# Four single feed-forward products by halves of the tokens, and a fifth PSUM bank for each pair of products

## The chip, the cores and the metric

The kernel runs on one core of a Trainium2 chip. The core has TensorE (PE in the rows; its weight loads are PEld), VectorE (DVE), ScalarE (ACT), GpSimd (POOL) and SyncE (SP, here only a DMA queue). The metric is device time of one execution in microseconds. The kernel before took 2143.89 us (median of 3 runs, 2141.85 to 2143.91).

## What is computed

One step of a two-layer backbone over 640 tokens of width 1024 (128 context tokens and 512 latent ones). Each layer has a token-mixing sub-layer and a SwiGLU feed-forward; the change is in the feed-forward alone:

```python
h = rms_norm(x, g_pre[1]) * (1 + sc2) + sh2
g, u = jnp.split(h @ w_ffn_in_l, 2, axis=-1)      # 1024 -> 2 x 2816
x = x + g2 * rms_norm((silu(g) * u) @ w_ffn_out_l, g_post[1])
```

All matrices are float32. The kernel splits each operand into a high and a low part of a shorter float format and adds three products (high by high, high by low, low by high), so each float32 product is three matmuls.

## The kernel before

**Tokens and weights.** The normalised input `h` stands transposed in `hT_hi` and `hT_lo` (128 partitions x 8 blocks of the width x 640 tokens). Tokens come in five tiles of 128, t0 to t4. `cut` places them so that the first half of the columns holds t1, t2 and half of t0, the second half the rest of t0 with t3 and t4. The 2816 columns of gate and up weights are 22 blocks of 128 each: `fg` (gate) and `fu` (up), n = 0 to 21. A block of weights arrives in a raw tile `wraw` (four of them) and is split by ACT (`whi`, the high part) and then DVE (`wlo`, the rest) into one of three slots of 1024 columns, or into one of two extra tiles `walt`, which lie in the memory called `m0` and `m1` (`alt_slot` says who uses which). `split_all` splits whatever next block finds a free slot, at the point of the program where a slot comes free; so the order of each engine's queue is set when the program is written out.

**The hand-over from the output projection.** `out_proj` computes its second half token tile by token tile. As a tile's last product ends, `tail` queues its residual, norm, transposes on PE (into `ps_t`), scale and shift (L609 on DVE for one half of the width, L611 on ACT for the other), and the split into `hT_hi` (L630, ACT) and `hT_lo` (L631; DVE does the first four blocks of the width, POOL the last four). These steps are deferred by a virtual clock (`defer`, `DELAYS`), and `run_tasks` puts them into the queues between products.

**Single products.** The first two blocks of each kind (n = 0, 1) are plain products of 24 matmuls for each half of the tokens (L650 to L652). The list `seq` is fg0, fu0, fg1, fu1. Before the change the first three go by halves: first half of the tokens for all three, then t3 and t4 have to be ready (`run_tasks(GTOK[1])`), then the second half; fu1 follows with both halves. Each result is drained from PSUM: ACT takes Silu for a gate (L1543), DVE multiplies for an up block (L1545) and the product is split into `aT` (L1547 on ACT, L1548 on DVE).

**Sums and pairs.** The other blocks go two at a time by a scheme of seven products of half the width by half the tokens (`pair`, 12 matmuls of 320 columns each, L744) in place of eight. It needs four sums of token blocks, S1 to S4, which `sums` makes from the normalised tokens in `nt` while the single products run: additions on DVE and POOL (L701, L705), then a split by ACT (L719) and DVE (L721). S1 is written to `m1`, S3 to `m0`, S2 to `o32`, S4 over the first four blocks of the second half of `hT`. `SUMS_AT` sets when each of the eight steps is put into the queues. The products take, in order: a block of `hT`, S2, S1, a block of `hT`, S3, S4, a block of `hT`.

**PSUM in a pair.** Six banks (`mm`) go round. Product 0 writes p1, copied out by ACT (L753); product 1 writes p2, read by DVE (L757, `u2 = p2 + m1`); product 2 writes p3, copied by ACT (L761). Product 3 is then added into p1, product 4 into p2 and product 5 into p3, each after that reader; product 6 has p4. DVE takes p2 again (L767), then p3 (L771) and p4 (L776). While the pairs of a layer run, DVE also does a slow side job, the modulation vectors of the next rounds (`ada_side`, L501 and L503).

Places in the program are named below by time. In layer 0 the single products start at 641 us and the first pair at 677 us; in layer 1 the same stretch starts at 1695.8 us and 1731.7 us. Each layer has 20 pairs: 4, 8 and 8, with a piece of the output product of the feed-forward after each.

Of the kernel before, what the change touches and what calls it, by code (L numbers as in the profile page):

```python
# [13 lines left out]
OP = mybir.AluOpType  # L14
# [10 lines left out]
HALVES = ((0, 320), (320, 640))  # L25
# [8 lines left out]
ADA_MIX = ([(0, 2), (0, 3), (0, 4)], [(1, 3), (1, 4)])  # L34
ADA_FFN = ([(0, 5), (1, 0), (1, 1), (1, 2)], [(1, 5)])
FFN_PARTS = (6, 8, 8)
SUMS_AT = (0.1, 0.2, 2.0, 3.0, 4.0, 5.0, 9.0, 99.0)
SUM_START, SUM_DT, SUM_ROWS = 5.0, 2.9, 256
TICK = 2.5
ADA_DT, ADA_LAG = (8.0, 1.8), 3  # L40
# [53 lines left out]
class Weights:  # L94
# [33 lines left out]
    @staticmethod  # L128
    def alt_slot(key):


        l, kind, n = key[:3]
        if kind in ("wo", "fo"):
            k0 = 0 if kind == "wo" else DFF // 128 - FFN_PARTS[-1]
            k1 = 6 if kind == "wo" else DFF // 128 - 2
            return {(0, k1): 0, (1, k0): 1}.get(key[2:])
        return 0 if n == 0 and (kind == "fg" or kind == "uc" and l) else None

    @staticmethod
# [148 lines left out]
class Kernel:  # L288
# [390 lines left out]
    def sums(self, z, offsets):  # L679

        nc, fix = self.nc, self.fix
        zv = z.rearrange("p t (k c) -> p t k c", c=128)
        tiles = {}

        blocks = ((1, 0), (1, 1), (2, 0), (2, 1), (0, 0)), ((0, 1), (3, 0), (3, 1), (4, 0), (4, 1))
        vec, pool = nc.vector.tensor_tensor, nc.gpsimd.tensor_tensor

        def pieces(half, kh):  # L690

            ks = slice(4 * kh, 4 * kh + 4)
            return zv[:, 1 + 2 * half:3 + 2 * half, ks, :], zv[:, 0, ks, 64 * half:64 * half + 64]

        def block(half, kh, i):
            t, b = blocks[half][i]
            return zv[:, t, 4 * kh:4 * kh + 4, 64 * b:64 * b + 64]

        def within(out, x, y, op):
            for i, (o, a, b) in enumerate(zip(*(pieces(*w) for w in (out, x, y)))):  # L700
                (pool if i else vec)(o, a, b, op=op)  # L701

        def across(out, x, y):
            for i in range(5):
                (pool if i in (1, 3) else vec)(*(block(*w, i) for w in (out, x, y)), op=OP.subtract)  # L705

        def store(name, at, tag):
            if tag is None:
                hi, lo = (w[:, 0:4, 320:640] for w in (self.hT_hi, self.hT_lo))
            else:  # L710
                s = fix.tile([128, 2, 4, 320], F32R, name=name, tag=tag, bufs=1)
                hi, lo = s[:, 0], s[:, 1]
            tiles[name] = hi, lo
            c = 64 * at[0]
            dh, dl = ((w[:, :, c:c + 256].rearrange("p k (t c) -> p t k c", t=2), w[:, :, 256 - 4 * c:320 - 4 * c])
                      for w in (hi, lo))
            src = pieces(*at)
            for o, a in zip(dh, src):
                nc.scalar.activation(o, a, AF.Copy)  # L719
            for o, a, b in zip(dl, src, dh):  # L720
                vec(o, a, b.bitcast(F32), op=OP.subtract)  # L721

        a11, a12, a21, a22 = (0, 0), (0, 1), (1, 0), (1, 1)
        steps = (lambda: within(a22, a21, a22, OP.subtract), lambda: across(a21, a11, a21),
                 lambda: store("S1", a22, "m1"), lambda: across(a11, a22, a11),
                 lambda: store("S2", a11, "o32"), lambda: within(a12, a12, a11, OP.add),
                 lambda: store("S3", a21, "m0"), lambda: store("S4", a12, None))
        for dt, f in zip(offsets, steps):
            self.defer(dt, f, "sums")
        h = lambda kh, half: tuple(w[:, 4 * kh:4 * kh + 4, 320 * half:320 * half + 320] for w in (self.hT_hi, self.hT_lo))  # L730
        self.left = (lambda: h(0, 0), lambda: tiles["S2"], lambda: tiles["S1"], lambda: h(1, 0), lambda: tiles["S3"],
                     lambda: tiles["S4"], lambda: h(1, 1))

    def pair(self, key, evac):

        nc, W = self.nc, self.W
        self.tmp = self.tmp[1], self.tmp[0], self.tmp[2]
        m1, u2, m5 = self.tmp
# [11 lines left out]
        psum = lambda: self.psum("mm")[:, :320]  # L750
# [2 lines left out]
        nc.scalar.activation(m1, p1, AF.Copy)  # L753
        end(0)
        p2 = psum()
        product(1, p2, True, False)
        nc.vector.tensor_tensor(u2, p2, m1, op=OP.add)  # L757
        end(1)
        p3 = psum()
# [3 lines left out]
        product(3, p1, False, True)  # L763
        evac(0, p1, 0)
        end(3)
        product(4, p2, False, True)
        nc.vector.tensor_tensor(m1, p2, m1, op=OP.add)  # L767
        nc.gpsimd.tensor_tensor(m5, m5, m1, op=OP.subtract)  # L768
        end(4)
        product(5, p3, False, True)  # L770
# [748 lines left out]
    def ffn(self, l):  # L1519
        nc = self.nc  # L1520
# [3 lines left out]
        for p, nt in enumerate(FFN_PARTS):  # L1524
# [27 lines left out]
            if p == 0:  # L1552
                first = FFN_SINGLE
                seq = [(kind, n) for n in range(first) for kind in ("fg", "fu")]
                self.tmp = [self.fp.tile([128, 320], F32, name=f"tmp{i}") for i in range(3)]
                for g in range(2):
                    self.run_tasks(GTOK[g])
                    if g:
                        self.sums(self.z, SUMS_AT)
                    for kind, n in seq[:3]:  # L1560
                        self.proj((l, kind, n), g, evac(kind, n), 4, HALVES)
                self.W.alt.clear()
                for kind, n in seq[3:]:
                    self.proj2((l, kind, n), evac(kind, n), HALVES)
                self.run_tasks(("sums",))
                rounds = ADA_FFN[l]
                self.run_tasks(range(5))
# [177 lines left out]
```

## Time and profile before

| | |
|---|---|
| time, median of 3 | 2143.89 us |
| the profiled execution | 2143.28 us |
| its span, first to last instruction | 2141.5 us |
| PE busy | 2089.6 us (98%) |
| DVE busy | 1237.4 us (58%) |
| ACT busy | 912.8 us (43%) |
| mean granted clock of PE | 0.995 |

The profile lists for each instruction its start, its length, and the idle time of its engine just before it with what ended that. A matmul of 320 columns is shown with a length of 0.31 us, but the next one starts 0.147 us after it: they overlap, so gaps between starts are read, not lengths. The profiled execution was 1.8 us longer than its span.

### The profile page before, as it was taken

The numbers are of one execution on the slowest core, as the hardware profiler recorded it, in microseconds if no ns is written. First come the engines' busy times: TensorE is split into PE (matmuls) and PEld (weight loads), VectorE is DVE, ScalarE is ACT, GpSimd is POOL, SyncE is SP. The second block draws the span as 40 slices with busy tenths as digits, with TensorE's granted clock in tenths as the row PEclk, the third lists the DMA queues.
The fourth block names the chain that finished last, engine by engine and source line by source line (L and its number), as shares of the span: only waits on it lengthen the run. The fifth ranks groups of instructions, "written<-read, shape, count | busy, mean of one in ns | idle before, by whom it ended". The sixth has DMA issues, their size and how long they took to land.

```text
span 2141.5 us, 35955 instructions
## 1 busy us (share of the span) xinstructions
PE 2089.6 (98%) x13876; PEld 1939.6 (91%) x13876; DVE 1237.4 (58%) x2289; ACT 912.8 (43%) x1947; POOL 515.1 (24%) x783
## 2 busy tenths in 40 slices
PE   6999999999999999999999999999999999999998
PEld 4999999998879889889889999999988798998996
DVE  3555664553357777777466556555533676563663
ACT  3644453432245434235356445434423543541541
POOL 3121325452123100100142124354321320010012
PEclk9999999999999999999999999999999999999999
DMA  8555769894644565554535466798855244442443
GB/s 277 153 115 147 162 194 187 212 212 137 224 157 140 178 186 166 175 162 142 195 110 143 128 150 168 191 195 202 185 177 197 99 141 146 139 148 79 138 153 123
DMA packets 369803, 349.68 MB, mean 163 GB/s; under 512 B 16608, under 2 KB 294144, under 8 KB 369376
## 3 DMA queue, kind: packets, MB, share of 16 engines
q1 hardware_dynamic: 337040, 293.51, 43.8%
q0 software_dynamic: 32160, 53.63, 14.5%
q8 instruction: 109, 1.79, 0.3%
q14 instruction: 62, 0.51, 0.1%
q10 hardware_dynamic: 432, 0.25, 0.0%
HBM read 335.50 MB, written 95.72 MB: 201 GB/s over the span
## 4 chain that ended last, share of the span: by engine, by line
PE 60%; DVE 3%; ACT 2%; POOL 2%; issue 1%; DMA 1%; DVEq 0%; POOLq 0%; ACTq 0%; SPq 0%
PE ps_mm L744 20%; PE ps_mm L650 7%; PE ps_mm L651 7%; PE ps_mm L652 6%; PE ps_mm L1406 5%; PE ps_mm L1408 5%; PE ps_mm L1407 5%; PE ps_t L842 1%; PE ps_o L856 1%; DMA vbt<-in_c_cvb 1%; PE ps_s L815 1%; PE ps_s L816 1%; POOL hT_lo L631 1%; ACT whi L172 1%; DVE wlo L173 0%
## 5 line engine op out<-in xcount | busy, mean ns | idle before, releaser
L173 DVE TENSOR_TENSOR wlo<-wraw,whi 128x512 fp32r<-128x512 f32 (+1 forms) x453 | 408.3, 908 | 406.8 <-ACT whi L172 401.4
L650 PE MATMUL ps_mm<-hT_hi,whi 128*128 128x256 f32 (+2 forms) x1552 | 489.3, 315 | 1.5 <-DVE sg L1369 1.0
L652 PE MATMUL ps_mm<-hT_hi,wlo 128*128 128x256 f32 (+2 forms) x1552 | 480.9, 310 | 0.7 <-DVE wlo L173 0.7
L651 PE MATMUL ps_mm<-hT_lo,whi 128*128 128x256 f32 (+2 forms) x1552 | 480.6, 310 | 0.0
L172 ACT ACTIVATE whi<-wraw 128x512 fp32r<-128x512 f32 (+1 forms) x453 | 354.4, 790 | 287.2 <-PE ps_mm L1408 147.1
L650 PEld LDWEIGHTS ps_mm<-hT_hi,whi 128*128 128x128 f32 x1552 | 292.6, 189 | 11.5 <-issue 7.2
L652 PEld LDWEIGHTS ps_mm<-hT_hi,wlo 128*128 128x128 f32 x1552 | 292.1, 188 | 1.2 <-DVE wlo L173 1.2
L651 PEld LDWEIGHTS ps_mm<-hT_lo,whi 128*128 128x128 f32 x1552 | 292.5, 188 | 0.4
L744 PE MATMUL ps_mm<-S,whi 128*128 128x320 f32 x960 | 212.8, 309 | 5.6 <-DVE tmp L757 5.6
L768 POOL TENSOR_TENSOR tmp<-tmp,tmp 128x320 f32<-128x320 f32 x40 | 53.5, 1336 | 652.3 <-DVE tmp L767 608.7
L744 PE MATMUL ps_mm<-hT_hi,whi 128*128 128x320 f32 x640 | 198.0, 309 | 1.4 <-ACT tmp L753 1.4
L744 PE MATMUL ps_mm<-hT_hi,wlo 128*128 128x320 f32 x640 | 197.3, 308 | 0.0
L744 PE MATMUL ps_mm<-hT_lo,whi 128*128 128x320 f32 x640 | 197.3, 308 | 0.0
L744 PEld LDWEIGHTS ps_mm<-S,whi 128*128 128x128 f32 x960 | 160.1, 188 | 7.1 <-DVE tmp L757 7.1
L1406 PE MATMUL ps_mm<-whi,aT 128*128 128x512 f32 x400 | 158.4, 396 | 0.0
L1408 PE MATMUL ps_mm<-whi,aT 128*128 128x512 f32 x400 | 157.9, 395 | 0.0
L1407 PE MATMUL ps_mm<-wlo,aT 128*128 128x512 f32 x400 | 157.8, 394 | 0.0
L744 PE MATMUL ps_mm<-S,wlo 128*128 128x320 f32 x480 | 148.1, 309 | 0.0
L744 PEld LDWEIGHTS ps_mm<-hT_hi,whi 128*128 128x128 f32 x640 | 120.1, 188 | 3.5 <-ACT tmp L753 2.5
L650 PE MATMUL ps_mm<-o,whi 128*128 128x256 f32 (+1 forms) x384 | 121.1, 315 | 0.0
L744 PEld LDWEIGHTS ps_mm<-hT_lo,whi 128*128 128x128 f32 x640 | 120.2, 188 | 0.2
L744 PEld LDWEIGHTS ps_mm<-hT_hi,wlo 128*128 128x128 f32 x640 | 120.1, 188 | 0.0
(236 smaller groups left out, 3893.8 us busy)
## 6 DMA issues: line engine op xcount, KB each, us to landing
wraw<-in_w_in SPq DMA_DIRECT2D x92, 512.0 KB, 4.3
wraw<-wsum SPq DMA_DIRECT2D x160, 256.0 KB, 3.3
wsum<-in_w_ffn_in POOLq DMA_DIRECT2D x64, 512.0 KB, 7.8
wraw<-in_w_ffn_in SPq DMA_DIRECT2D x120, 256.0 KB, 3.4
wraw<-in_w_ada SPq DMA_DIRECT2D x56, 512.0 KB, 3.8
wraw<-in_w_ffn_out SPq DMA_DIRECT2D x44, 512.0 KB, 4.1
ada_side<-in_w_ada SPq DMA_DIRECT2D x40, 512.0 KB, 3.8
wsum<-in_w_ffn_in SPq DMA_DIRECT2D x32, 512.0 KB, 6.7
```

What stands on the lines that cost most here:

```text
L172: self.k.nc.scalar.activation(hi, src, AF.Copy)
L173: self.k.nc.vector.tensor_tensor(lo, src, hi.bitcast(F32), op=OP.subtract)
L631: (lo_on or (nc.gpsimd if q else nc.vector)).tensor_tensor(lo, zq, hi.bitcast(F32), op=OP.subtract)
L650: nc.tensor.matmul(ps, wh, xh[:, c0:c1], start=(k == 0), stop=False)
L651: nc.tensor.matmul(ps, wh, xl[:, c0:c1], start=False, stop=False)
L652: nc.tensor.matmul(ps, wl, xh[:, c0:c1], start=False, stop=(k == K - 1))
L744: nc.tensor.matmul(ps, w[p][:, k, :], x[q][:, k, :], start=first and k == 0 and j == 0, stop=last and k == 3 and j == 2, skip_group_check= ...
L768: nc.gpsimd.tensor_tensor(m5, m5, m1, op=OP.subtract)
L815: nc.tensor.matmul(out, u["q"][:, h, u["qc"]], u["khi"](h), start=True, stop=False)
L1406: nc.tensor.matmul(ps, xh, u.hi[:, i, :], start=st and i == 0, stop=False)
L1407: nc.tensor.matmul(ps, xh, u.lo[:, i, :], start=False, stop=False)
L1408: nc.tensor.matmul(ps, xl, u.hi[:, i, :], start=False, stop=sp and i == 1)
```

## The change

Three edits go together. All four single products now go by halves: fg0, fu0, fg1 and fu1 for the first half of the tokens, then all four for the second. fu0 is split into the second extra tile `walt`, in `m1`, and no longer into one of the three slots; S1 moves to `m0`, S3 to `m1`, and four times in `SUMS_AT` move back. And the pair's product 4 no longer adds into p2: it has a bank of its own, p5, and DVE computes `m1 = p5 + u2` instead of `p2 + m1` (the sum is the same). No instruction is added or dropped except that two splits of 1024 columns are now four of 512.

```diff
-SUMS_AT = (0.1, 0.2, 2.0, 3.0, 4.0, 5.0, 9.0, 99.0)
+SUMS_AT = (0.1, 0.2, 3.3, 4.0, 5.0, 6.0, 9.0, 99.0)
...
+        if n == 0 and kind == "fu":
+            return 1
         return 0 if n == 0 and (kind == "fg" or kind == "uc" and l) else None
...
-                 lambda: store("S1", a22, "m1"), lambda: across(a11, a22, a11),
+                 lambda: store("S1", a22, "m0"), lambda: across(a11, a22, a11),
                  lambda: store("S2", a11, "o32"), lambda: within(a12, a12, a11, OP.add),
-                 lambda: store("S3", a21, "m0"), lambda: store("S4", a12, None))
+                 lambda: store("S3", a21, "m1"), lambda: store("S4", a12, None))
...
         p2 = psum()
-        product(1, p2, True, False)
+        product(1, p2, True, True)
...
-        product(4, p2, False, True)
-        nc.vector.tensor_tensor(m1, p2, m1, op=OP.add)
+        p5 = psum()
+        product(4, p5, True, True)
+        nc.vector.tensor_tensor(m1, p5, u2, op=OP.add)
...
-                    for kind, n in seq[:3]:
+                    for kind, n in seq:
                         self.proj((l, kind, n), g, evac(kind, n), 4, HALVES)
                 self.W.alt.clear()
-                for kind, n in seq[3:]:
-                    self.proj2((l, kind, n), evac(kind, n), HALVES)
```

In the changed file the lines stand 2 or 3 further down (L609 is L611, L173 is L175, L719 is L721, L753 is L755).

The queue of DVE in layer 0, where the output projection hands over to the single products. `nt` holds the tokens, `ps_t` their transposes, and the rows from L609 (L611) on are those of tile t2. Before:

```order
L590 TENSOR_SCALAR nt<-x,ss 128x1024
L631 TENSOR_TENSOR hT_lo<-nt,hT_hi 128x4x128
L1513 TENSOR_TENSOR nt<-ps_mm,gm 128x512
L609 TENSOR_SCALAR nt<-ps_t,a_0_6195,sh_0_6032 128x128 x4
L1483 SCALAR_TENSOR_TENSOR x<-nt,ss,x 128x1024
L631 TENSOR_TENSOR hT_lo<-nt,hT_hi 128x4x128
L173 TENSOR_TENSOR wlo_272<-wraw,whi_271 128x1024
L173 TENSOR_TENSOR wlo_270<-wraw,whi_269 128x1024
L590 TENSOR_SCALAR nt<-x,ss 128x1024
L173 TENSOR_TENSOR wlo_268<-wraw,whi_267 128x1024
```

And of the changed kernel:

```order
L592 TENSOR_SCALAR nt<-x,ss 128x1024
L633 TENSOR_TENSOR hT_lo<-nt,hT_hi 128x4x128
L1516 TENSOR_TENSOR nt<-ps_mm,gm 128x512
L175 TENSOR_TENSOR walt<-wraw,walt 128x1024
L611 TENSOR_SCALAR nt<-ps_t,a_0_6195,sh_0_6032 128x128 x4
L1486 SCALAR_TENSOR_TENSOR x<-nt,ss,x 128x1024
L633 TENSOR_TENSOR hT_lo<-nt,hT_hi 128x4x128
L175 TENSOR_TENSOR wlo_272<-wraw,whi_271 128x1024
L175 TENSOR_TENSOR wlo_270<-wraw,whi_269 128x1024
L592 TENSOR_SCALAR nt<-x,ss 128x1024
L175 TENSOR_TENSOR wlo_268<-wraw,whi_267 128x512 x2
```

The split of fu0 has moved from one of the slots into `walt`, which is free earlier: it now stands in front of t2's scale and shift. The two halves at the end are the first two parts of the first pair.

The queue of ACT in layer 0 just ahead of the first pair (`aT` drains fu1; the rows `hT_hi<-nt` are S4; the first `tmp` row is the copy of product 0 out of p1, the second that of product 2 out of p3). Before:

```order
L1547 ACTIVATE aT_6640<-sg 128x320 x2
L172 ACTIVATE whi_267<-wraw 128x512 x2
L719 ACTIVATE hT_hi<-nt 128x2x4x128
L719 ACTIVATE hT_hi<-nt 128x4x64
L753 ACTIVATE tmp_6645<-ps_mm 128x320
L172 ACTIVATE whi_271<-wraw 128x512 x2
L761 ACTIVATE tmp_6646<-ps_mm 128x320
```

And of the changed kernel:

```order
L1550 ACTIVATE aT_6647<-sg 128x320
L174 ACTIVATE whi_269<-wraw 128x512 x2
L721 ACTIVATE hT_hi<-nt 128x2x4x128
L721 ACTIVATE hT_hi<-nt 128x4x64
L755 ACTIVATE tmp_6652<-ps_mm 128x320
L174 ACTIVATE whi_267<-wraw 128x512 x2
L763 ACTIVATE tmp_6653<-ps_mm 128x320
```

The order is the same, but only one drain of fu1 (its second half) stands here; the other has moved ahead of the sums, and PE has one half product less to do before the first pair.

## Rows read from the trace of the kernel before

**Rows 1.** The head of the page: the span, and the busy time of each engine.

```profile
span 2141.5 us, 35955 instructions
PE 2089.6 (98%) x13876; PEld 1939.6 (91%) x13876; DVE 1237.4 (58%) x2289; ACT 912.8 (43%) x1947; POOL 515.1 (24%) x783
```

**Rows 2.** The view of waits, PE alone: who waited for whom, us in total, times, longest.

```profile
PE ps_mm L744 <- DVE tmp L757: 5.6, 6, 1.3
...
PE ps_mm L650 <- ACT hT_hi L630: 4.1, 3, 1.9
```

**Rows 3.** The timeline of PE over the single products of layer 0 (start, length, idle before it and what ended it in brackets): the second matmul of the first half, the wait in the first half, the last matmul of the first half, the first of the second half, the thirteenth of it, the first of fu0 and of fg1 in the second half. The last row is layer 1's first matmul of the second half.

```profile
641.33 0.41 PE L651 MATMUL ps_mm<-hT_lo,walt 128*128 128x320 f32 x1
...
644.73 0.42 PE L651 MATMUL ps_mm<-hT_lo,walt 128*128 128x320 f32 x1 [1.38 <-POOL hT_lo L631]
...
655.19 0.31 PE L652 MATMUL ps_mm<-hT_hi,wlo 128*128 128x320 f32 x1
657.36 0.46 PE L650 MATMUL ps_mm<-hT_hi,walt 128*128 128x320 f32 x1 [1.85 <-ACT hT_hi L630]
...
661.11 0.31 PE L650 MATMUL ps_mm<-hT_hi,walt 128*128 128x320 f32 x1
...
662.87 0.31 PE L650 MATMUL ps_mm<-hT_hi,whi 128*128 128x320 f32 x1
...
666.39 0.31 PE L650 MATMUL ps_mm<-hT_hi,whi 128*128 128x320 f32 x1
...
1712.08 0.45 PE L650 MATMUL ps_mm<-hT_hi,walt 128*128 128x320 f32 x1 [1.85 <-ACT hT_hi L630]
```

**Rows 4.** The view of stretches, 658 to 661 us and 770.5 to 872 us (the eight pairs of layer 0's second part): start and end, length, then busy time of PE, PEld, DVE, ACT and POOL, PE's granted clock (0.5 is 1.2 GHz, 1.0 is 2.4 GHz), DMA share, GB/s.

```profile
658.00:661.00 3.00, 2.91 (x11) 2.92 (x12) 1.83 (x3) 0.02 (x1) 1.87 (x2) 0.50 0.00 0
770.50:872.00 101.50, 98.44 (x674) 96.59 (x673) 74.25 (x124) 49.26 (x100) 11.14 (x12) 1.00 0.57 167
```

**Rows 5.** The timeline of DVE around the first half: the low part of t2, a split of 1024 columns, and the low part of t4.

```profile
640.59 0.68 DVE L631 TENSOR_TENSOR hT_lo<-nt,hT_hi 128x512 fp32r<-128x512 f32 x1
...
646.34 1.22 DVE L173 TENSOR_TENSOR wlo<-wraw,whi 128x1024 fp32r<-128x1024 f32 x1
...
657.34 0.69 DVE L631 TENSOR_TENSOR hT_lo<-nt,hT_hi 128x512 fp32r<-128x512 f32 x1 [0.47 <-ACT hT_hi L630]
```

**Rows 6.** The timeline of POOL: its share of the low part of t2 and of t4.

```profile
640.23 4.45 POOL L631 TENSOR_TENSOR hT_lo<-nt,hT_hi 128x512 fp32r<-128x512 f32 x1 [1.95 <-ACT hT_hi L630]
...
657.90 1.27 POOL L631 TENSOR_TENSOR hT_lo<-nt,hT_hi 128x512 fp32r<-128x512 f32 x1 [4.29 <-ACT hT_hi L630]
```

**Rows 7.** The timeline of DVE through the sums: the first addition, the second (POOL works on its part at the same time), the last addition, the drain of fu0, four splits for the pair, S3's low part, the last drain of fu1.

```profile
659.20 1.75 DVE L701 TENSOR_TENSOR nt<-nt 128x1024 f32<-128x1024 f32 x1 [1.17 <-POOL hT_lo L631]
...
668.92 1.22 DVE L701 TENSOR_TENSOR nt<-nt 128x1024 f32<-128x1024 f32 x1
670.06 0.48 DVE L1545 TENSOR_TENSOR sg<-sg,ps_mm 128x320 f32<-128x320 f32 x1
...
671.60 2.66 DVE L173 TENSOR_TENSOR wlo<-wraw,whi 128x512 fp32r<-128x512 f32 x4
674.44 1.56 DVE L721 TENSOR_TENSOR S<-nt,S 128x1024 fp32r<-128x1024 f32 x2 [0.18 <-ACT S L719]
...
677.35 0.48 DVE L1545 TENSOR_TENSOR sg<-sg,ps_mm 128x320 f32<-128x320 f32 x1
```

**Rows 8.** The timeline of ACT from the last drain of fu1 to the copy out of p1.

```profile
677.86 0.47 ACT L1547 ACTIVATE aT<-sg 128x320 fp32r<-128x320 f32 x1 [0.95 <-DVE sg L1545]
...
679.28 1.34 ACT L719 ACTIVATE hT_hi<-nt 128x1024 fp32r<-128x1024 f32 x2
680.54 0.42 ACT L753 ACTIVATE tmp<-ps_mm 128x320 f32<-128x320 f32 x1
```

**Rows 9.** The timeline of PE: the first matmul of the first pair, and of its product 3.

```profile
676.95 0.31 PE L744 MATMUL ps_mm<-hT_hi,whi 128*128 128x320 f32 x1
...
682.23 0.31 PE L744 MATMUL ps_mm<-hT_hi,whi 128*128 128x320 f32 x1
```

**Rows 10.** The timeline of DVE in the first pair: the first step of the side job.

```profile
688.08 0.75 DVE L501 TENSOR_SCALAR ada_side<-ada_side,ada_st 128x1024 f32<-128x1024 f32 x1 [0.92 <-DMA ada_side<-in_w_ada]
```

**Rows 11.** The timeline of ACT: the copy out of p1 in the third pair of layer 0 and in the seventh.

```profile
706.43 0.42 ACT L753 ACTIVATE tmp<-ps_mm 128x320 f32<-128x320 f32 x1
...
802.08 0.42 ACT L753 ACTIVATE tmp<-ps_mm 128x320 f32<-128x320 f32 x1
```

**Rows 12.** The view of waits, PE alone, in two stretches: 770.5 to 872 us (the eight pairs of layer 0's second part) and 931.7 to 1034 us (its third part).

```profile
PE ps_mm L744 <- DVE tmp L757: 2.1, 2, 1.3
...
PE ps_mm L744 <- DVE tmp L757: 1.8, 2, 1.0
```

**Rows 13.** The timeline of PE: product 4 of the fifth pair, product 3 and product 4 of the seventh.

```profile
778.99 0.56 PE L744 MATMUL ps_mm<-S,whi 128*128 128x320 f32 x2 [1.29 <-DVE tmp L757]
...
802.55 0.41 PE L744 MATMUL ps_mm<-hT_hi,whi 128*128 128x320 f32 x1 [0.42 <-ACT tmp L753]
...
805.39 0.56 PE L744 MATMUL ps_mm<-S,whi 128*128 128x320 f32 x2 [0.82 <-DVE tmp L757]
```

**Rows 14.** The timeline of DVE in the fifth pair: the read of p2, and its next turn, after product 4.

```profile
778.45 0.49 DVE L757 TENSOR_TENSOR tmp<-ps_mm,tmp 128x320 f32<-128x320 f32 x1
...
781.06 0.49 DVE L767 TENSOR_TENSOR tmp<-ps_mm,tmp 128x320 f32<-128x320 f32 x1 [0.32 <-PE ps_mm L744]
```

## The prediction

> **What bounds the kernel now.** I read the page first, then PE's waits, then the timeline where they are. PE is busy 98% of the span [rows 1], so the change can give back only time in which PE waits or runs at half clock. The view of waits lists it [rows 2]: the two causes that the edits touch are the start of the second half of the tokens (PE on `hT_hi`, 4.1 us in three waits, two of them here) and product 4 of a pair (PE on L757, 5.6 us in six waits). The last matmul of the first half starts at 655.19 in layer 0 and the next one could start at 655.34, 0.147 us later. It starts at 657.36, and the thirteenth only at 661.11 [rows 3], for PE's granted clock has fallen to 0.5, which is 1.2 GHz of 2.4 [rows 4]. Thirteen matmuls on time would have reached 655.34 + 12 x 0.147 = 657.10, so the place costs 4.0 us. Layer 1 shows the same wait of 1.85 us [rows 3]. Elsewhere PE hardly waits for what is changed, so this is a matter of some 14 us in 2143.
>
> **Four products by halves, what it takes away.** A half product lasts 666.39 - 662.87 = 3.52 us [rows 3]. With fu1's first half put ahead of the second half, PE comes to t3 and t4 3.52 us later. The late operand is t4's low part, ready at 657.34 + 0.69 = 658.03 [rows 5] when PE would have wanted it at 655.34 + 0.15. POOL's share is ready at 657.90 + 1.27 = 659.17 [rows 6] and is wanted only by the second four blocks, 1.76 us after. So 2.7 us are missing, 3.52 are offered, the wait goes, and with it the fall of the clock: minus 4.0 us for each layer, if nothing comes after it.
>
> **What it adds ahead.** fu0's split into `walt` now stands in DVE's queue before t2's scale and shift (order above). DVE has no gap there; a split of 1024 columns takes 1.22 us [rows 5]. The low part of t2 ended at 640.59 + 0.68 = 641.27, and PE took it up at 641.33 [rows 3, 5]: no cover at all. So PE waits 1.2 us longer there. POOL's share of t2, after which the 1.38 us wait at 644.73 ends [rows 3, 6], follows the same scale and shift and moves by the same 1.2, so that wait keeps its length; the tails of t3 and t4 come behind it and move as well. ACT's half of the split costs nothing: ACT stood idle there for its next transposes. Plus 1.2 us for each layer. Bounds: 0 (the split fits a gap) and 1.2 + 1.9 (two waits so near each other lower the clock once more, priced like the fall above, 4.0 less its waits of 2.1). I take 1.2, since one wait of 1.38 did not lower it.
>
> **What comes late next.** PE would then begin the second half at 655.34 + 1.2 + 3.52 = 660.06 and the first pair after four halves, at 674.1, against 676.95 [rows 9]: 2.8 us earlier. But the sums wait for DVE, and DVE hardly gains. After t4 it now drains fu1's first half (ready on PE at 660.3; drain 671.60 - 670.06 = 1.54 us with ACT's turn in between), then does the chain from L701 to the drain of fu0, 670.06 - 659.20 = 10.86 us, less 0.6 because POOL's first piece is out of the way (1.75 against 1.22), then that drain (1.54), two splits (2.66 / 2), S3 (0.18 + 1.56), and the last drain's first step (0.48) [rows 7]: 16.9 us, to 677.2. Before, that step ended at 677.83. From there ACT drains, splits two parts, splits S4, and only then copies p1: 680.96 - 677.83 = 3.1 us [rows 7, 8]. So p1 is free at 680.3. PE wants to add product 3 into it at 674.1 + 3 x 1.76 = 679.4 and waits 0.9 us; S4 and the weights are ready in time. Product 3 of the first pair starts at 680.35 in place of 682.23 [rows 9]: of the 2.8 us, 1.9 are left. The Trainium skill ("SBUF — State Buffer", "Who interferes with whom") says that DVE with two SBUF inputs and a GpSimd instruction that reads SBUF exclude each other, and that the one that started second is blocked until the other ends. Rows agree in kind (POOL 1.27 alone, 4.45 beside DVE [rows 6]). If POOL alone were the one blocked in the sums, DVE's chain would be shorter and the 0.9 us wait would go, 1.8 us off the sum in both layers; the sum keeps the contended rows.
>
> **The bank for product 4.** Its wait for L757 goes. The third pair of each layer has one of 0.82 (what rows 12 and two pieces of that size leave of the 5.6), layer 0's later pairs 2.1 and 1.8 [rows 2, 12]. But PE then runs into the next reader on the same two engines: product 3 waits for the copy out of p1. In layer 0's seventh pair that copy ends at 802.50, and product 3 already waits for it [rows 11, 13]. Without the 1.29 at 778.99 PE would be there 1.45 earlier (the wait and the overlap lost with it). DVE is not: between its read of p2 at 778.45 and its turn at 781.06 it has only 0.32 us of idle time [rows 14], and I allow as much again in the sixth pair. So the copy ends 0.65 earlier, product 3 gains 0.65, product 4 then gains 0.82 + 0.15: 1.6 us in layer 0's second part. The third part has the same two waits and the same side job, 1.6. In the third pair of each layer the copy stands at 706.43 [rows 11], also just in time. PE comes 1.9 earlier, DVE about 1.05 (0.75 as the side job's first step waits for its DMA [rows 10], which is issued that much earlier behind the weights' loads, and 0.3 of idle time); so product 3 keeps 1.05 of the 1.9, and product 4 adds 0.82 + 0.2. That is 2.1 us for each layer up to there. The new bank itself costs nothing: with five banks a pair, a bank comes round after six takings, that is more than one pair (12.3 us) later, and its readers are done within some 5 us.
>
> **Sum.** Layers' starts 2 x 2.1 = 4.2, layer 0's later pairs 1.6 + 1.6 = 3.2, together 7.4 us. The profiled execution, 2143.28 with 1.8 us outside its span of 2141.5, would become 2135.9; the median of 2143.89 becomes **2136.5 us**.
>
> **Rivals.**
> 1. *The waits only move.* DVE's chain in the sums is 1.9 us longer than reckoned (its additions meet POOL at other places: 0.5 to 1.1 us a piece by rows 7, 1.75 against 1.22, up to POOL's 3.2 [rows 6]), and each saved wait on L757 comes back at L753. Then the starts give nothing and the pairs 1 to 2 us: 2142. For it: both readers are fed by the same two engines, and PE waits on both in one pair [rows 13].
> 2. *Nothing comes late next.* DVE's idle times absorb all: 2 x (4.0 - 1.2 + 1.0) + 3.9 + 0.6 = 12.1 us less: 2131.8. Against it: the p1 copy is just in time already [rows 11, 13].
> 3. *Slower: the sums are held up on DVE by POOL.* If S2, the second L701 and both shares of t4's low part meet the other engine as t2's did (POOL 3.2 us more [rows 6], DVE 0.5 to 1.1 a piece), the chain is 5 to 6 us longer, product 3 of the first pair starts at 686 instead of 682.23, and both layers lose 4, less 1 by the third pair's bank and 3.2 in layer 0: 2146. It decides from 1.9 us a layer for the starts alone, from about 3.5 for the whole.
> 4. *The clock.* Each fall costs some 1.9 us beyond the wait. If the more frequent change of banks made PE pause often enough to fall once in each of the 40 pairs, 2136.5 + 76 = 2212. Against it: layer 0's second eight pairs hold waits of 1.29, 0.82 and 0.42 us, and their granted clock is 1.00 throughout [rows 4, 12, 13]. The Trainium skill ("TensorE: Matmul & The Clock Gate", "A second HAM failure mode: psum-queue depth-cycling") describes such a case, a matmul kernel that went round its PSUM banks and paid for falls of the clock between bursts; no row here shows one.
>
> **How the numbers follow.** The forecast, 2133 to 2139.5, has 0.63; rival 1, 2139.6 to 2143, 0.19; rival 2, below 2133, 0.11; rival 3 0.06; rival 4 0.01. Some 0.2% (4.3 us) is about what a measurement of this kernel can tell from no change. Faster by more than that is below 2139.6: 0.63 + 0.11 = 0.74, less 0.02 for the forecast's edge, 0.72; within it 0.19 + 0.02 = 0.21; slower 0.06 + 0.01 = 0.07, though rival 3 at its mildest would still lie within it. The range that leaves out 2 in 10 goes from rival 2's 2131.5 to rival 1's 2141.8.
>
> **What would show it.** Right: no wait of `hT_hi` at the second half and PE's clock at 1.0 there; a longer wait, some 1.2 us, at the second matmul of the first half; a wait of about 0.9 us of product 3 in the first pair on the copy out of p1; no wait on the read of p2; waits on that copy of 0.9 to 1.4 us in the third pair of each layer and in layer 0's seventh and fifteenth. Wrong: the half clock at 644 us; a wait of product 5 for S4; or product 3's waits gone.

## The result, and the profile after

The changed kernel takes **2131.18 us** (median of 4, 2129.98 to 2131.83) beside 2143.9 us of the kernel before on the same chip (2141.85 to 2144.85): ratio 0.9943, interval 0.9929 to 0.9957, so 12.7 us less. Timed once more later (label after_again): 2132.29 beside 2142.24 us, ratio 0.9951, interval 0.9939 to 0.9964, 10.0 us less by these medians. The forecast was 2136.5 us, 7.4 us less, with a range from 2131.5 to 2141.8: the sign was right, the size too small, and the first median lies 0.3 us below the range, among the times below 2133 us that the forecast had left to rival 2 with a chance of 0.11.

PE's waits in the changed kernel, the three groups that answer to the edits (total us, times, longest; L755 is the copy out of p1, L633 the low part of `hT`). The row of [rows 2] for L757 has no successor here: product 4 waits for nothing. Of the row for `hT_hi`, 4.1 us in three waits, one wait of 0.4 is left, at the start of layer 1 (1088 us): the second half waits for nothing. DVE's wait of 1.2 us is at the start of layer 1 too and was there before; the other two are the edit's.

```profile
PE ps_mm L746 <- ACT tmp L755: 3.3, 6, 1.1
PE ps_mm L653 <- DVE hT_lo L633: 3.3, 3, 1.2
...
PE ps_mm L653 <- POOL hT_lo L633: 2.7, 2, 1.4
...
PE ps_mm L652 <- ACT hT_hi L632: 0.4, 1, 0.4
```

The timeline of PE in layer 0, answering to [rows 3, 9, 13]: the second matmul of the first half, the wait for POOL, the last matmul of the first half (now fu1's), the first of the second half, the first of the first pair, the last of its product 2 and the first of its product 3, and product 3 of the third, the seventh and the fifteenth pair.

```profile
641.37 0.41 PE L653 MATMUL ps_mm<-hT_lo,walt 128*128 128x320 f32 x1 [1.07 <-DVE hT_lo L633]
...
644.77 0.41 PE L653 MATMUL ps_mm<-hT_lo,walt 128*128 128x320 f32 x1 [1.37 <-POOL hT_lo L633]
...
658.75 0.31 PE L654 MATMUL ps_mm<-hT_hi,wlo 128*128 128x320 f32 x1
658.90 0.31 PE L652 MATMUL ps_mm<-hT_hi,walt 128*128 128x320 f32 x1
...
672.98 0.31 PE L746 MATMUL ps_mm<-hT_hi,whi 128*128 128x320 f32 x1
...
678.10 0.31 PE L746 MATMUL ps_mm<-S,wlo 128*128 128x320 f32 x1
678.61 0.41 PE L746 MATMUL ps_mm<-hT_hi,whi 128*128 128x320 f32 x1 [0.20 <-ACT tmp L755]
...
704.03 0.41 PE L746 MATMUL ps_mm<-hT_hi,whi 128*128 128x320 f32 x1 [0.54 <-ACT tmp L755]
...
797.66 0.41 PE L746 MATMUL ps_mm<-hT_hi,whi 128*128 128x320 f32 x1 [1.06 <-ACT tmp L755]
...
956.58 0.42 PE L746 MATMUL ps_mm<-hT_hi,whi 128*128 128x320 f32 x1 [0.76 <-ACT tmp L755]
```

The view of stretches (columns as in [rows 4]): the two waits of the first half, and the start of the second.

```profile
641.00:646.00 5.00, 3.26 (x20) 3.00 (x21) 2.88 (x4) 4.98 (x9) 4.75 (x5) 1.00 0.74 246
658.00:661.00 3.00, 3.00 (x23) 3.00 (x22) 1.50 (x4) 0.47 (x1) 1.98 (x2) 1.00 0.00 0
```

Read together: the second half now starts 0.147 us after the first ends, at a granted clock of 1.00. In exchange the second matmul of the first half waits 1.07 us for DVE, and what is left in the pairs is product 3 waiting for the copy out of p1.

**Lengths of stages.** To compare executions I take the starts of PE's matmuls and subtract: from the first matmul of the single products to the first of the first pair (start), then groups of pairs. A group that has a piece of the output product behind it ("pairs 2-4" and "part 2") includes that piece; "part 3" ends with the last matmul of its pairs. Row "before" gives the length in us in the profiled execution, the others their difference from it. "Up to start 0" is time before layer 0's single products, where nothing is edited but the place of fu0's split, in its last 3 us; "between" runs from layer 0's last pair to layer 1's single products.

| kernel | up to start 0 | start 0 | pair 1 | pairs 2-4 | part 2 | part 3 | between | start 1 | pair 1 | pairs 2-4 |
|---|---|---|---|---|---|---|---|---|---|---|
| before | 641.09 | 35.86 | 12.31 | 81.24 | 161.23 | 102.58 | 661.49 | 35.85 | 12.31 | 81.24 |
| before_again | +1.36 | -1.30 | +0.44 | -0.01 | 0.00 | -0.01 | -0.02 | +0.24 | 0.00 | 0.00 |
| after | -1.10 | -2.87 | +0.46 | -0.45 | -2.01 | -2.02 | -0.04 | -2.89 | +0.51 | -0.87 |
| after_again | +0.21 | -2.88 | +0.50 | -0.31 | -2.01 | -2.00 | -1.45 | -2.88 | +0.51 | -0.64 |
| bank_alone | -0.91 | -1.31 | +0.25 | -0.63 | -1.99 | -2.02 | -1.58 | -0.05 | 0.00 | -1.09 |
| halves_alone | +0.43 | -2.86 | +0.73 | +1.16 | 0.00 | -0.01 | -1.59 | -2.87 | +0.72 | -0.01 |
| fu0_held | +2.26 | -1.37 | +0.49 | -0.63 | -2.01 | -2.01 | -1.23 | -1.38 | +0.49 | -0.62 |
| t2_on_dve | -0.39 | -3.61 | +0.49 | -0.31 | -2.01 | -2.02 | +0.08 | -3.63 | +0.50 | -1.09 |
| held_t2 | +1.12 | -3.64 | +0.49 | +0.08 | -2.01 | -2.01 | -1.61 | -3.62 | +0.50 | -0.61 |
| copy_first | -2.12 | -2.86 | +0.50 | -1.25 | -4.07 | -3.05 | -0.01 | -2.86 | +0.50 | -1.25 |
| copy_s4 | +0.06 | -2.87 | -0.01 | -1.25 | -4.04 | -3.05 | +0.02 | -2.87 | 0.00 | -1.25 |
| t2_copy_s4 | +0.06 | -3.63 | -0.01 | -1.25 | -4.07 | -3.05 | -1.59 | -3.62 | +0.01 | -1.25 |

Layer 1's later pairs have the same length everywhere, the tail after them within 0.34 us. The columns under an edit add to 10.1 us less for after and 9.7 for after_again. The other two columns move between executions, whatever the kernel: "up to start 0" from 2.1 us less to 2.3 more, "between" from 1.6 less to 0.1 more. Of the 11.5 us between the two profiled spans (2141.5 and 2130.0), 1.1 came from the first of them.

"Between" has two levels, and the granted clock tells them apart. In the token mixing of layer 1 PE waits for DVE in every profile, 2.16 to 2.43 us. In six of the twelve the clock then falls to half (before, before_again, after, t2_on_dve, copy_first, copy_s4), and these six agree within 0.1 us. In the other six it stays, and the column is 1.2 to 1.6 us shorter. The wait and the stretch behind it, in after and in after_again:

```profile
1410.10 0.33 PE L845 MATMUL ps_t<-ident,P 128*128 128x128 f32 x1 [2.18 <-DVE P L835]
...
1411.67 0.33 PE L845 MATMUL ps_t<-ident,P 128*128 128x128 f32 x1 [2.18 <-DVE P L835]
```

```profile
1411.00:1414.00 3.00, 3.00 (x10) 2.99 (x11) 2.02 (x5) 1.48 (x5) 1.92 (x2) 0.50 1.12 205
...
1412.50:1415.50 3.00, 3.00 (x17) 2.82 (x17) 2.02 (x5) 1.55 (x5) 1.93 (x2) 1.00 1.14 208
```

### The profile page after: what moved, and what is told of

It reads as the page before. It is cut to its first block, busy times and chain, and to the rows that moved or that the text cites. A ratio compares the mean times of both kernels' runs of the same rounds, so it can differ in the third digit from the quotient of the medians.

```text
span 2130.0 us, 35991 instructions
## 1 busy us (share of the span) xinstructions
PE 2082.0 (98%) x13876; PEld 1934.9 (91%) x13876; DVE 1232.7 (58%) x2289; ACT 911.7 (43%) x1947; POOL 513.3 (24%) x783
## 4 chain that ended last, share of the span: by engine, by line
PE 60%; DVE 4%; ACT 2%; POOL 2%; issue 2%; DMA 1%; DVEq 0%; POOLq 0%; ACTq 0%
PE ps_mm L746 20%; PE ps_mm L652 6%; PE ps_mm L653 6%; PE ps_mm L654 6%; PE ps_mm L1409 5%; PE ps_mm L1411 5%; PE ps_mm L1410 5%; PE ps_o L859 1%; PE ps_t L845 1%; PE ps_s L818 1%; DMA wsum<-in_w_ffn_in 1%; PE ps_s L819 1%; POOL hT_lo L633 1%; ACT whi L174 1%; DVE wlo L175 1%
## 5 line engine op out<-in xcount | busy, mean ns | idle before, releaser
L175 DVE TENSOR_TENSOR wlo<-wraw,whi 128x512 fp32r<-128x512 f32 (+1 forms) x451 | 404.7, 905 | 404.5 <-ACT whi L174 399.9
L652 PE MATMUL ps_mm<-hT_hi,whi 128*128 128x384 f32 (+2 forms) x1520 | 478.7, 315 | 1.8 <-DVE sg L1372 1.0
L654 PE MATMUL ps_mm<-hT_hi,wlo 128*128 128x384 f32 (+2 forms) x1520 | 470.7, 310 | 1.4 <-DVE wlo L175 1.4
L653 PE MATMUL ps_mm<-hT_lo,whi 128*128 128x384 f32 (+2 forms) x1520 | 470.3, 309 | 0.0
L652 PEld LDWEIGHTS ps_mm<-hT_hi,whi 128*128 128x128 f32 x1520 | 286.2, 188 | 11.1 <-issue 7.2
L654 PEld LDWEIGHTS ps_mm<-hT_hi,wlo 128*128 128x128 f32 x1520 | 285.9, 188 | 1.9 <-DVE wlo L175 1.9
L653 PEld LDWEIGHTS ps_mm<-hT_lo,whi 128*128 128x128 f32 x1520 | 286.0, 188 | 0.4
L746 PEld LDWEIGHTS ps_mm<-hT_hi,whi 128*128 128x128 f32 x640 | 120.1, 188 | 6.3 <-ACT tmp L755 5.3
L746 PEld LDWEIGHTS ps_mm<-hT_lo,whi 128*128 128x128 f32 x640 | 120.1, 188 | 0.2
L746 PEld LDWEIGHTS ps_mm<-hT_hi,wlo 128*128 128x128 f32 x640 | 120.1, 188 | 0.0
```

What stands on the lines that cost most here:

```text
L175: self.k.nc.vector.tensor_tensor(lo, src, hi.bitcast(F32), op=OP.subtract)
L652: nc.tensor.matmul(ps, wh, xh[:, c0:c1], start=(k == 0), stop=False)
L653: nc.tensor.matmul(ps, wh, xl[:, c0:c1], start=False, stop=False)
L654: nc.tensor.matmul(ps, wl, xh[:, c0:c1], start=False, stop=(k == K - 1))
L746: nc.tensor.matmul(ps, w[p][:, k, :], x[q][:, k, :], start=first and k == 0 and j == 0, stop=last and k == 3 and j == 2, skip_group_check= ...
```

## The experiments

**1. bank_alone**: the kernel before with the fifth bank only.

```diff
-        product(1, p2, True, False)
+        product(1, p2, True, True)
...
-        product(4, p2, False, True)
-        nc.vector.tensor_tensor(m1, p2, m1, op=OP.add)
+        p5 = psum()
+        product(4, p5, True, True)
+        nc.vector.tensor_tensor(m1, p5, u2, op=OP.add)
```

> The kernel before with the fifth bank alone; the single products stay as they were. Theory A (each wait of product 4 on the read of p2 goes with the overlap that it cost, and in the third pairs nothing comes late next because PE is not early there): third pair of each layer 1.25 us shorter, layer 0's second and third part 2.0 us each: 6.5 us less, about 2137.4 beside 2143.9. Theory B (the waits only move to product 3 and the copy out of p1): at most 2 us less, about 2142. The start of the second half keeps its 4 us loss in both.

Measured 2134.26 us, ratio 0.9953 (0.9940 to 0.9965). Parts 2 and 3 give 2.0 us each, as A said, the first four pairs of each layer 0.4 and 1.1 us where A had 1.25: 5.5 us in the pairs, of 9.3 by the medians. In the waits L757 is gone, and L753, which had 1.4 us in three waits, has

```profile
PE ps_mm L744 <- ACT tmp L753: 2.7, 4, 1.1
```

So part of the saved time moves on to product 3, not all of it: B is out. Unforeseen was layer 0's start, 1.3 us shorter with no edit there. Two matmuls that start the second half, in layer 0 and layer 1 of this kernel, and the stretch behind each:

```profile
656.45 0.41 PE L650 MATMUL ps_mm<-hT_hi,walt 128*128 128x320 f32 x1 [1.85 <-ACT hT_hi L630]
...
1703.88 0.61 PE L650 MATMUL ps_mm<-hT_hi,walt 128*128 128x320 f32 x1 [1.87 <-ACT hT_hi L630]
```

```profile
657.00:660.00 3.00, 2.83 (x19) 2.83 (x20) 1.80 (x3) 0.00 (x0) 1.98 (x2) 1.00 0.00 0
1704.00:1707.00 3.00, 2.88 (x10) 2.54 (x11) 1.82 (x2) 0.34 (x1) 1.96 (x2) 0.50 0.00 0
```

The same wait, but the clock fell only in the second. In this profile the fall missing in layer 0 and the one missing in "between" make 2.9 us that come from the clock and not from the pairs, and the way up to start 0 was 0.9 us shorter. Why the median too is 3.8 us further down than the pairs say stays open.

**2. halves_alone**: the changed kernel with product 4 added into p2 again.

```diff
-        product(1, p2, True, True)
+        product(1, p2, True, False)
...
-        p5 = psum()
-        product(4, p5, True, True)
-        nc.vector.tensor_tensor(m1, p5, u2, op=OP.add)
+        product(4, p2, False, True)
+        nc.vector.tensor_tensor(m1, p2, m1, op=OP.add)
```

> The changed kernel with product 4 added into p2 again; only the four half products, the placing of fu0's split and the sums stay. Theory A (the loss at the second half was 2.0 us of wait and 1.9 us of half clock, and both go): each layer reaches its first pair 2.9 us earlier, the pair waits on L757 come back on top of the waits for p1's copy: 3.5 to 5 us less than before, about 2139.5. Theory B (only the wait itself was lost, the clock's fall is paid elsewhere): 1 us for each layer, 2142, with a fall of the granted clock still near the first pairs.

Measured 2138.97 us, ratio 0.9979 (0.9969 to 0.9989). The starts keep their 2.9 us, but pairs 1 to 4 of layer 0 give back 1.9 of it (0.73 + 1.16) and layer 1's 0.7. The edited columns add to 3.1 us, and those of bank_alone, with layer 0's start left out, to 5.5: together 8.6, less than the 10.1 of both at once. The two edits need each other: the earlier start only arrives at a wait for p2, unless the bank is there. The moved times in `SUMS_AT` and the exchange of `m0` and `m1` go with the halves in every run here; what they do alone is not shown. The waits in the pairs are

```profile
PE ps_mm L746 <- DVE tmp L759: 5.5, 6, 1.3
...
PE ps_mm L746 <- ACT tmp L755: 2.5, 6, 0.6
```

**3. fu0_held**: the changed kernel, with fu0's split held until t2's low part is queued.

```diff
-            elif slot not in self.alt:
+            elif slot not in self.alt or u.key[1] == "fu" and not self.fu_open:
...
-        self.defer(d_split, lambda: self.pre_t2(sub, t, z, (0, 1)), t)
+        def split():
+            self.pre_t2(sub, t, z, (0, 1))
+            if sub and t == 2:
+                self.W.fu_open = True
+                self.W.split_all()
+        self.defer(d_split, split, t)
...
```

Two more lines set `fu_open` to False, at the start and in `out_proj`.

> The changed kernel with fu0's split into walt queued right behind t2's low part in place of ahead of t2's scale and shift. Theory A (that split is the 1.07 us wait at the second matmul): the wait of 1.07 goes in both layers, the 1.37 for POOL stays, and product 3 of the first pair waits up to 0.8 us longer for the copy out of p1, since DVE's sums come only in part earlier: 0.6 to 2.1 us less than the changed kernel. Theory B (the wait for POOL's share grows by as much, because three splits of DVE now lie beside it): no difference.

Measured 2134.93 us, ratio 0.9955 (0.9941 to 0.9968). The wait of 1.07 us went, as A said, but the other grew by as much, as B said, and, foreseen by neither, each start is 1.5 us *longer* than in the changed kernel. DVE and POOL of this kernel at t2's low part, and PE's wait with the stretch behind it:

```profile
643.46 1.22 DVE L175 TENSOR_TENSOR walt<-wraw,walt 128x1024 fp32r<-128x1024 f32 x1
644.60 2.35 DVE L175 TENSOR_TENSOR wlo<-wraw,whi 128x1024 fp32r<-128x1024 f32 x2
```

```profile
642.49 5.58 POOL L633 TENSOR_TENSOR hT_lo<-nt,hT_hi 128x512 fp32r<-128x512 f32 x1 [1.94 <-ACT hT_hi L632]
```

```profile
648.13 0.41 PE L653 MATMUL ps_mm<-hT_lo,walt 128*128 128x320 f32 x1 [2.50 <-POOL hT_lo L633]
```

```profile
649.00:652.00 3.00, 3.00 (x14) 2.96 (x14) 2.82 (x5) 1.04 (x4) 1.15 (x3) 0.50 0.94 276
```

POOL's share needs 1.27 us when alone [rows 6] and ends 1.1 us after DVE's last split, at 648.07 against 646.95. One wait of 2.50 us lowered the clock in both layers; 1.07 and 1.37 us in the changed kernel, with nearly the same sum, did not. But for 0.06 us by which the waits differ, the 1.5 us is the price of that fall.

**4. t2_on_dve** and **5. held_t2**: POOL's share of t2's low part given to DVE, in the changed kernel and in fu0_held.

```diff
-        self.defer(d_split, lambda: self.pre_t2(sub, t, z, (0, 1)), t)
+        self.defer(d_split, lambda: self.pre_t2(sub, t, z, (0, 1), nc.vector if sub and t == 2 else None), t)
```

> The changed kernel with POOL's share of t2's low part given to DVE, right behind DVE's own share. Theory A (POOL took 4.45 us only because DVE's splits held it up, and PE's 1.37 us wait is for that alone): DVE needs 0.6 us more there, the wait of 1.37 goes, the 1.07 ahead of it stays; since the sums come 0.7 us later or at the old time, the first pair's product 3 waits longer: 1 to 2.5 us less than the changed kernel in both layers together. Theory B (DVE's queue is what PE waits for throughout, and 0.6 us more in it moves t3, t4 and the sums back): no difference or up to 1 us more.

> Both of it: t2's low part wholly on DVE, and fu0's split into walt behind it. Theory A (holding fu0 failed because POOL's share went from 4.45 to 5.58 us beside three splits of DVE, and the clock fell after the wait of 2.5 us): both waits of the first half go, 2.4 us in each layer, but t4 is then wanted at 656.7 where it is ready at about 658: a wait of 1 to 1.5 us comes back at the second half; 1 to 4 us less than the changed kernel. Theory B (holding costs by itself, since fu0 comes late): slower than the changed kernel by 1 us or more, with a wait on walt.

Measured 2131.11 us, ratio 0.9941 (0.9929 to 0.9954), and 2133.84 us, ratio 0.9952 (0.9939 to 0.9964). In both the wait for POOL is gone and each start is 0.74 us shorter than in the changed kernel; neither median shows that gain. What comes late next is not t4, as I had expected of held_t2, but PE's transposes of t3: 0.74 us in t2_on_dve, and 1.88 in held_t2, whose PE comes to them without an earlier wait:

```profile
646.48 0.33 PE L604 MATMUL ps_t<-ident,nt 128*128 128x128 f32 x1 [0.74 <-DVE nt L592]
```

```profile
647.98 0.33 PE L604 MATMUL ps_t<-ident,nt 128*128 128x128 f32 x1 [1.88 <-DVE nt L592]
```

Their scaled rows (L592, DVE) do not stand behind the splits in DVE's own queue; DVE is idle for 0.77 us before them, waiting for POOL's part of the norm of t3. POOL's first step there (L569), which takes 0.22 us in the changed kernel, lasts 1.06 us beside the splits and ends at 644.98, just after the last split at 644.90. In t2_on_dve, first DVE and then POOL:

```profile
642.55 2.35 DVE L175 TENSOR_TENSOR wlo<-wraw,whi 128x1024 fp32r<-128x1024 f32 x2
645.67 0.75 DVE L592 TENSOR_SCALAR nt<-x,ss 128x1024 f32<-128x1024 f32 x1 [0.77 <-POOL ss L572]
```

```profile
643.92 1.06 POOL L569 TENSOR_SCALAR ss<-ss 128x1 f32<-128x1 f32 x1 [6.03 <-ACT nt L587]
```

In held_t2 that step lasts 1.25 us and again ends 0.1 us after the last split. Holding fu0 bought nothing either way: in both orders POOL's step for t3 comes behind all three splits, and the starts have the same length within 0.03 us.

**6. copy_first**: the last drain of a pair is queued behind the next pair's copy out of p1.

```diff
         nc.scalar.activation(m1, p1, AF.Copy)
+        self.flush()
         end(0)
...
-        evac(1, m5, 1)
+        self.late = lambda: evac(1, m5, 1)
         end(6)
...
```

`flush` runs what `late` keeps; it is also called once behind the last pair of a part.

> The changed kernel with the last drain of each pair queued behind the next pair's copy out of p1 instead of ahead of it, on ACT and DVE. Theory A (what is left in the pairs, 4.9 us over 12.31 us each, is product 3 waiting for ACT, which stands in the drains' turns with DVE): the waits on L755 go except in the first pairs: 3.5 to 4.5 us less than the changed kernel, about 2127. Theory B (ACT and DVE are simply behind, the wait goes over to product 5 and the copy out of p3, or to the weights): within 1 us of the changed kernel.

Measured 2127.83 us, ratio 0.9923 (0.9910 to 0.9935). Every pair but the first of each layer is within 0.13 us of 12.31 us, apart from layer 0's eleventh and twelfth, in which PE does a piece of the side job in every run (13.51 and 12.53 us), and of the waits on the copy only the first pairs' are left (the copy stands at L760 here):

```profile
PE ps_mm L751 <- ACT tmp L760: 0.5, 2, 0.2
```

A holds: ACT was not short of time, the copy stood behind drains that take turns with DVE.

**7. copy_s4**: S4's step too goes behind the first copy.

```diff
-                self.run_tasks(("sums",))
+                self.late = lambda: self.run_tasks(("sums",))
```

> copy_first with S4's step also queued behind the first copy out of p1. Theory A (in the first pair of a layer the copy stands behind S4's split on ACT): the first pairs come back to 12.31 us, 0.5 us less in each layer than copy_first: 1 us less, no wait left in a pair. Theory B (the copy waits for fu1's last drain, which DVE delays): no difference; or S4 is late for product 5.

Measured 2126.59 us, ratio 0.9918 (0.9904 to 0.9931). The first pairs are at 12.31 us, and no product of any pair waits any more. A holds.

**8. before_again**, the kernel before unchanged.

> The kernel before as it is, for a second profile. Theory A (the stretches that no edit touches vary by 1 to 3 us between executions, the stages' own lengths don't): pairs and other stretches of the same length within 0.05 us, the start up to 641 us and the stretch around 1097 us off by up to 2 us. The half clock at the second half of the tokens: theory A says that it falls in both layers again; theory B (the fall depends on more than the wait, since the kernel with the bank alone shows the same wait of 1.85 us in layer 0 with no fall) says that it is missing in one or both, and that start is 1.3 us shorter.

Measured 2143.81 us. The pairs agree within 0.01 us, but for layer 0's first, which gave back 0.44 of an earlier start. The starts follow B: the wait is there in both layers, the half clock only in layer 1.

```profile
658.73 0.41 PE L650 MATMUL ps_mm<-hT_hi,walt 128*128 128x320 f32 x1 [1.87 <-ACT hT_hi L630]
```

```profile
659.00:662.00 3.00, 2.69 (x18) 2.54 (x18) 1.80 (x2) 0.20 (x1) 1.99 (x2) 1.00 0.00 0
1713.50:1716.50 3.00, 3.00 (x12) 3.00 (x12) 2.10 (x3) 0.33 (x1) 1.84 (x3) 0.50 0.00 0
```

**9. after_again** and **10. t2_copy_s4**: the changed kernel unchanged, and copy_s4 with t2's low part on DVE.

> The changed kernel as it is, for a second profile and a time beside t2_copy_s4 on the same chip. Theory A (the stages that the edits touch repeat to 0.05 us): starts of 33.0 us and pairs as in its first profile, no half clock between 641 and 677 us; time 2131 to 2133. Theory B (that its clock did not fall there was chance, as in one of four places of the kernel before and the one with the bank alone): a fall after the waits of 1.07 and 1.37 us, and a start 1.3 us longer in one or both layers.

> copy_s4 with t2's low part wholly on DVE as well. Theory A (with no wait left in the pairs the earlier start is kept): starts of 32.25 us as in t2_on_dve, pairs of 12.31 us as in copy_s4: 1.5 us less than copy_s4, about 2125. Theory B (the first pairs take the 0.75 back, since the sums are no earlier): the time of copy_s4.

after_again repeats the edited stages within 0.25 us, again with no fall in either start: A on the clock, though pairs 2-4 differ by 0.14 and 0.23 us where A had allowed 0.05. t2_copy_s4 took 2125.93 us, ratio 0.9926 (0.9912 to 0.9939). Its starts and pairs are those that A named, 1.5 us less than copy_s4 in the stages, but the times of the two cannot be told apart. Both beat both kernels of this case: 16 to 17 us less than before, some 5 to 6 less than the changed one.

## Why the prediction was right, and where its sizes were off

**The start of the second half**: right. The wait is gone, the clock is at 1.00 there, and the start to the first pair is 2.87 and 2.89 us shorter; forecast 2.8 (4.0 less 1.2). But the 4.0 is the price in an execution whose clock fell. Without a fall the start of the kernel before is 34.56 us instead of 35.86 (before_again), so the fall is 1.3 us and not the 1.9 that I had as the rest of 4.0. The other 0.7 us go with the short second wait behind the first: without a fall the first product of the second half still takes 4.21 us (658.73 to 662.94 in before_again) in place of 3.52. Beside an execution without the fall, layer 0's start gains 1.3 us less, of which the first pair, itself 0.44 us longer there, makes up a part.

```profile
662.94 0.31 PE L650 MATMUL ps_mm<-hT_hi,whi 128*128 128x320 f32 x1
```

**fu0's split ahead of t2**: right, 1.07 us waited against 1.2. The bound that two waits so near would lower the clock once more did not come true in any of the ten starts that have the two waits (after, after_again, halves_alone, copy_first, copy_s4); fu0_held shows that one wait of their sum does.

**What comes late next**: the right wait, too large. Product 3 of the first pair should wait 0.9 us for the copy out of p1; it starts 678.61 - 678.10 - 0.147 = 0.36 us late (the first two numbers in the timeline above), with 0.1 us behind it, and the pair is 0.46 longer. I had set DVE's chain from t4 to the last drain 0.65 us too long: two splits and S3 took 1.29 and 1.55 us with no wait, the first drain came 0.2 earlier:

```profile
659.10 0.49 DVE L1548 TENSOR_TENSOR sg<-sg,ps_mm 128x320 f32<-128x320 f32 x1 [0.96 <-PE ps_mm L654]
...
660.53 1.22 DVE L703 TENSOR_TENSOR nt<-nt 128x1024 f32<-128x1024 f32 x1
...
672.28 1.29 DVE L175 TENSOR_TENSOR wlo<-wraw,whi 128x512 fp32r<-128x512 f32 x2
673.49 1.55 DVE L723 TENSOR_TENSOR S<-nt,S 128x1024 fp32r<-128x1024 f32 x2
674.96 0.48 DVE L1548 TENSOR_TENSOR sg<-sg,ps_mm 128x320 f32<-128x320 f32 x1
```

From there the 3.1 us to the end of the copy were right (675.44 to 678.56):

```profile
678.15 0.41 ACT L755 ACTIVATE tmp<-ps_mm 128x320 f32<-128x320 f32 x1
```

That S4's split on ACT makes this wait is shown by copy_s4.

**The bank, third pairs**: the size of a term. "Product 3 keeps 1.05 of the 1.9, and product 4 adds 0.82 + 0.2" gave 2.1 us up to there; measured 2.86 in layer 0 and 3.25 in layer 1 (2.69 and 3.01 in after_again). About half a microsecond of it is the shorter wait in the first pair, the rest the third pair itself. The "1.05" was too low: in layer 0 the third pair's copy out of p1 ended at 706.85 before and ends at 703.98 now, and with the 1.10 us by which this execution reached start 0 earlier taken off it came 1.77 us earlier.

```profile
703.56 0.42 ACT L755 ACTIVATE tmp<-ps_mm 128x320 f32<-128x320 f32 x1
```

**The bank, layer 0's later pairs**: the step "DVE is not: ... 0.32 us of idle time, and I allow as much again" was too low. It put the copy of the seventh pair 0.65 us earlier. That copy ended at 802.50 before, with the fifth pair started at 770.50; now the fifth pair starts 3.96 us earlier, and the copy

```profile
797.19 0.42 ACT L755 ACTIVATE tmp<-ps_mm 128x320 f32<-128x320 f32 x1
```

ends at 797.61, which is 802.50 - 3.96 - 797.61 = 0.93 earlier. Product 4's wait had cost 1.08 us and not the 0.97 that I took: after its wait of 0.82 the first matmul started 0.98 us late, and the next 0.10 later again. Together that makes 2.0 and not 1.6 us. The third part gains the same, though its two waits were 0.98 and 0.82 and not "the same two" [rows 12].

**The signs.** The full clock at the second half, the wait at the second matmul and the end of the wait on p2 came as named; none of the three signs of being wrong came. The waits on the copy were mostly shorter: 0.20 us for 0.9 in the first pair; for 0.9 to 1.4, 0.54 in layer 0's third pair and none that the view of waits lists in layer 1's, 1.06 in the seventh and 0.76 in the fifteenth.

**The sum**: 0.2 us more from the starts, 0.8 from the first pairs, 0.9 from the third, 0.8 from the later parts: 10.1 for 7.4. So the mechanism was right, and the gains of all four terms were set too small. The rest of the first result's 12.7 cannot be given to the change: the stretches without edits vary by 1 to 2 us an execution, and the repeat gave 10.0.

**The rivals.** That the waits only move is refuted by bank_alone and by the starts. That nothing comes late next was nearest in time, and is still wrong: 5.2 us of longer pairs were left, which copy_first and copy_s4 took out. No run shows the sums held up by POOL for 5 us, or a fall of the clock in the pairs.

**The rule on DVE and POOL.** POOL is not the only one that is blocked, so the contended rows were the right ones to reckon with. At t3 POOL's share began first, and DVE's, 0.68 us at t2, took 1.77 (first POOL, then DVE, in the changed kernel):

```profile
651.96 1.77 POOL L633 TENSOR_TENSOR hT_lo<-nt,hT_hi 128x512 fp32r<-128x512 f32 x1 [0.16 <-ACT hT_hi L632]
```

```profile
652.50 1.77 DVE L633 TENSOR_TENSOR hT_lo<-nt,hT_hi 128x512 fp32r<-128x512 f32 x1
```

At t2 it is POOL that waits. The first row is POOL, the others DVE:

```profile
640.27 4.45 POOL L633 TENSOR_TENSOR hT_lo<-nt,hT_hi 128x512 fp32r<-128x512 f32 x1 [3.08 <-ACT hT_hi L632]
```

```profile
639.45 1.27 DVE L1486 SCALAR_TENSOR_TENSOR x<-nt,ss,x 128x1024 f32<-128x1024 f32 x1
640.64 0.68 DVE L633 TENSOR_TENSOR hT_lo<-nt,hT_hi 128x512 fp32r<-128x512 f32 x1
641.24 2.35 DVE L175 TENSOR_TENSOR wlo<-wraw,whi 128x1024 fp32r<-128x1024 f32 x2
```

DVE's splits keep 1.2 us each, as anywhere; POOL ends 1.1 us after the last of them, and after one split more in fu0_held again 1.1 us after the last. The Trainium skill ("SBUF — State Buffer", "Who interferes with whom") has the instruction that comes second blocked until the other ends. The trace agrees at t3, and at t2 for the first instruction, L1486, which was running when POOL's began. For the rest it differs: POOL's was there at 640.27, before DVE's low part (640.64) and its splits (641.24), and still ended behind them all. POOL's times are rough; that it ended 1.1 us after the last split, with two and with three of them, is what shows that it did not get in between DVE's instructions while these followed each other without a gap.

## What to carry to other kernels

A step that frees time and one that lets the next stage take it are worth more together than apart: here 10.1 us against 3.1 and 5.5. When a wait is taken away, ask which instruction on the releasing engine stands ahead of the next one that PE needs; queueing that one first (the copy ahead of a drain and of S4's split) gave a further 5 us for two moved calls. For effects of 1 us compare lengths of stages between fixed instructions, look whether a stretch that nobody edited had a fall of the clock in one execution and not in the other, and take a second profile of the same kernel before giving a difference a cause.

## What was unexpected of the hardware

- The fall of PE's granted clock is not fixed by the wait alone. The same wait of 1.85 to 1.88 us at the second half, with one of 0.1 to 0.3 behind it, was followed by the half clock in 4 of 6 places (before: both layers; before_again and bank_alone: layer 1 only). The wait of 1.88 and 1.90 us at t3's transposes in held_t2 was followed by it in none of 2, one of 2.50 us (fu0_held) in 2 of 2, 1.07 and 1.37 us in a row in none of 10, and the wait in layer 1's token mixing, 2.16 to 2.43 us, in 6 of 12. A fall cost 1.2 to 1.6 us.
- A POOL instruction of 1.27 us lasted 4.45 and 5.58 us beside two and three back-to-back splits of DVE, with the same two DVE instructions ahead of these, and in each case ended 1.1 us after the last one. One of 0.22 us lasted 1.06 and 1.25 in the same way.
- Between executions layer 1's later pairs repeat to 0.02 us, and so do layer 0's from the second on between the two profiles of the kernel before, while the start of the program moved by 4.4 us (from 2.1 less to 2.3 more) and "between" by 1.2 to 1.6 with the clock.
